# A fp32 two-layer attention and convolution trunk: softmax's division moved into a tanh gate, and another order of the first loads

## The chip, the cores and the metric

The program runs on one core of one Trainium2 chip. The metric is the device time of one execution in microseconds (us). The engines that matter here are TensorE (PE in the rows, with PEld for its weight loads), VectorE (DVE), ScalarE (ACT), GpSimd (POOL) and SyncE (SP), whose queue issues nearly all DMAs.

## What is computed

The input x has 256 tokens of 2048 channels, fp32. Layer 0 is attention, layer 1 a convolution module, and only layer 0 is touched by the change. Cut to what matters:

```
h = x * rsqrt(mean(x*x) + eps) * norm_g          # per token
proj = h @ a_w_in                                # 2048 -> 9*2048 (q, k, v of 3 groups) + 2048 (z)
for each group g of 3, head of 16:
    q, k = q * rsqrt(mean(q*q)) * q_gain, k * rsqrt(mean(k*k)) * k_gain
    s = q k^T / sqrt(128) + bias[bucket(distance), head], masked by the group's window
    o_g = softmax(s) v,   lse_g = log-sum-exp of s
o = sum over g of softmax(lse)_g * o_g           # = one softmax over the three groups' scores
y = o * silu(z)                                  # silu(z) = z / (1 + exp(-z))
x = x + y @ a_w_out
```

As the three groups are merged by their log-sum-exp, one softmax over 512 columns of scores (256 of group 0, 128 each of groups 1 and 2) per token and head gives o. Then comes layer 1 (input projection, gated convolution over 31 taps, layer norm, output projection), and the residual.

## The kernel before, in words

**Weights.** Everything is fp32, computed as three products of fp32r halves: each operand is split into a high part (`hi`, `xh`) and the rest (`lo`, `xl`), and hi·hi, lo·hi and hi·lo are summed in PSUM. The weights come as 480 chunks of 128x1024 (512 KB). `stage(n)` (L101) issues the DMA of chunk n on SP's queue into `raw`, has ScalarE write `hi` and VectorE (or GpSimd, `low_engine`) write `lo`; `raw`, `hi` and `lo` have five buffers each. The main loop (L814) stages chunk n + 3 (`LEAD`), multiplies chunk n, and then runs what `at(n, ...)` had entered for step n. So each engine's program order is that of the steps: chunk n + 3's split, then the helpers of step n.

**Layer 0's projection.** Chunks 0 to 319 go through `project` (L246): 12 matmuls of 512 columns each, the three products of a 128-row block one after the other for token half b = 0 and then b = 1. Eight chunks make one column group (a 512-wide accumulator for each token half), five groups make a set of two heads (`hs`, 8 sets): q and k of the three attention groups, then v, then v and z.

**The first loads.** `load_x(c)` (L140) loads two 128-row blocks of x (256 KB), writes `xh` on ScalarE and `xl` on VectorE, and sums squares on GpSimd: a product (L158) and one or two sums (L160 to L163) per pair of blocks. It is called before `stage` for chunks 0 to 7, all on SP's queue. `warm_up` (L165) runs 16 transposes of an identity and one Exp at the start. `first_norm` (step 8) sums the squares over the channels with one-column matmuls (`token_sums`) and makes r0 = rsqrt(mean).

**Attention.** The helpers of a set run beside the next set's chunks. With e the set's last step: `z_take` at e + 1 copies z (scaled by r0), `z_gate` at e + 2 and e + 3 (token halves) makes z / (1 + exp(-z)) with an Exp on ScalarE and an addition, a reciprocal and a product on VectorE; `z_turn` and `z_put` at e + 4 and e + 5 transpose and copy it. Four units (head, token half) start at t = e + 3, e + 6, e + 9 and e + 12: `scores` at t, `softmax` (bias, maximum, Exp with its sum) at t + 1, `weigh` at t + 2 (reciprocal of the sum on VectorE, then GpSimd multiplies the 128x512 `pr` by it), `turn` at t + 3 (four transposes of `pr` into PSUM), `split` at t + 4 (hi and lo halves of it). Each head's second unit is followed by `values` (t + 5), `gated` (t + 6) and `y_split` (t + 7). The last set has t = e + 1, e + 3, e + 5, e + 7, beside the first chunks of the output projection (`project_out`, 24 matmuls of 256 columns a chunk), where GpSimd writes `lo`. The PSUM tag "t" has two buffers; `scores` (its second half), `turn`, `qk_turn`, `z_turn` and the bias rows take them in turn, each waiting until the one two earlier has been read.

**Bias rows.** In set 0, four times, `bias_load`, `bias_split`, `bias_rows` (two halves) and `bias_store` at steps 8, 10, 11, 12 and 13 (then each 6 later) compute the relative bias and write it to DRAM by SP's queue. The store waits there for VectorE's sum, and the next `bias_load` overwrites the same row buffer.

Of the kernel before, what the change touches and what calls it, by code (L numbers as in the profile page):

```python
# [17 lines left out]
P = 128  # L18
# [23 lines left out]
def hybrid_kernel(ctx: ExitStack, tc: tile.TileContext, x_perm, x_nat, vecs, rel, onehot, maskrow,  # L42
# [85 lines left out]
    yh = bpool.tile([P, NH, S], F32R, tag="yh", name="yh")  # L128
    yl = bpool.tile([P, NH, S], F32R, tag="yl", name="yl")
# [6 lines left out]
    nr0 = cpool.tile([P, 2], F32, name="nr0")  # L136
    gqk = cpool.tile([P, NG], F32, name="gqk")
    ssx = apool.tile([P, S], F32, name="ssx")

    def load_x(c):  # L140

        xr = apool.tile([P, 2, S], F32, tag=("sc", "pr")[c % 2], name=f"xr{c}", bufs=2)
        if c == 0:
            stage(0, 2)
            nc.sync.dma_start(xr[:, 0:1], x_perm[:, 0:1, :])
            nc.sync.dma_start(vec[:, :V_HEAD], vecs[:, :V_HEAD])
        else:
            nc.sync.dma_start(xr, x_perm[:, c * 2:(c + 1) * 2, :])
        for i in range(2):
            k = c * 2 + i  # L150
            if k == 1:
                nc.sync.dma_start(xr[:, 1:2], x_perm[:, 1:2, :])
            g0 = vec[:, V_G0 + k:V_G0 + k + 1]
            nc.scalar.activation(xh[:, k, :], xr[:, i, :], AF.Copy, scale=g0)  # L154
            nc.vector.scalar_tensor_tensor(xl[:, k, :], xr[:, i, :], g0, xh[:, k, :].bitcast(F32),  # L155
                                           op0=ALU.mult, op1=ALU.subtract)
        sq = apool.tile([P, 2, S], F32, tag="sq", name=f"xsq{c}", bufs=2)
        nc.gpsimd.tensor_tensor(sq, xr, xr, op=ALU.mult)  # L158
        if c == 0:
# [86 lines left out]
    def project(n):  # L246
# [146 lines left out]
    def values(st, h):  # L393
# [20 lines left out]
    def gated(st, h):  # L414
# [5 lines left out]
        nc.vector.tensor_tensor(st.y, st.y, st.gz[:, h, :, :], op=ALU.mult)  # L420

    def y_split(st, h):
# [3 lines left out]
        hi = yh[:, head, :].rearrange("p (i f) -> p f i", f=4)  # L426
        lo = yl[:, head, :].rearrange("p (i f) -> p f i", f=4)
# [486 lines left out]
```

## Time and profile before

| | us |
|---|---|
| median of 3 runs (range) | 1473.94 (1473.72 to 1475.07) |
| the profiled execution's own time | 1472.46 |
| its span, first to last instruction | 1470.7 |
| TensorE busy in it | 1448.6 |
| VectorE, ScalarE, GpSimd busy | 988.7, 721.6, 493.2 |

The page's lines by engine give busy times as shares of the span; the waits name who released an engine that sat idle; the timeline gives instructions in order of time, in us from the span's start. A busy time of TensorE is modelled and its matmuls overlap, so the pace is read from the distance of their starts.

### The profile page before, as it was taken

What the parts mean: (1) busy time and instruction counts of PE and PEld (TensorE: products, weight loads), DVE (VectorE), ACT (ScalarE), POOL (GpSimd) and SP (SyncE); (2) the same over time, 40 slices, a digit from 0 to 9 for tenths busy, and PEclk for the clock granted to TensorE, in tenths of its full rate; (3) what the DMA queues carried; (4) which work ended last, traced back from release to release, by engine and by line L of the source; (5) the groups of instructions that cost most, each with busy time, mean ns of one, the idle gap of its engine ahead of it and who ended that gap; (6) DMA issues with size and microseconds to landing.
All of it is one profiled execution on the core that took longest, in us unless ns stands there. A gap on an engine that the chain in (4) does not pass through costs nothing.

```text
span 1470.7 us, 22547 instructions
## 1 busy us (share of the span) xinstructions
PE 1448.6 (98%) x8556; PEld 1277.8 (87%) x8556; DVE 988.7 (67%) x1542; ACT 721.6 (49%) x1011; POOL 493.2 (34%) x394
## 2 busy tenths in 40 slices
PE   8999999999999999999999999999999999999999
PEld 6778888888788888888878888889999999999999
DVE  8656765775675676577567567655658989998621
ACT  5444554454454455445445445544544545455732
POOL 7210220210030022021003002207316979998544
PEclk9999999999999999999999999999999999999999
DMA  7458457457456645745745664566465655555544
GB/s 254 156 185 261 153 188 215 147 170 223 162 160 194 198 154 184 217 150 167 224 159 166 190 201 149 186 170 228 158 201 166 201 180 172 184 190 175 185 161 140
DMA packets 108124, 269.20 MB, mean 183 GB/s; under 512 B 42352, under 2 KB 44656, under 8 KB 108016
## 3 DMA queue, kind: packets, MB, share of 16 engines
q1 hardware_dynamic: 108016, 267.76, 57.6%
q8 instruction: 67, 1.10, 0.3%
q14 instruction: 41, 0.34, 0.1%
HBM read 265.36 MB, written 2.36 MB: 182 GB/s over the span
## 4 chain that ended last, share of the span: by engine, by line
PE 93%; DVE 2%; POOL 2%; ACT 1%; DMA 1%; issue 1%; SPq 0%; ACTq 0%; POOLq 0%; DVEq 0%
PE acc L257 19%; PE acc L259 19%; PE acc L258 18%; PE b L508 6%; PE b L509 6%; PE b L510 6%; PE psq L294 1%; POOL pr L377 1%; ACT hi L109 1%; DMA raw<-w_in 1%; PE vo L510 1%; PE vo L509 1%; PE vo L508 1%; PE vow L496 1%; PE vow L495 1%; PE vow L493 1%
## 5 line engine op out<-in xcount | busy, mean ns | idle before, releaser
L109 ACT CAST hi<-raw 128x1024 fp32r<-128x1024 f32 (+1 forms) x481 | 497.4, 1045 | 297.5 <-PE acc L258 165.3
L110 DVE TENSOR_TENSOR lo<-raw,hi 128x1024 fp32r<-128x1024 f32 (+1 forms) x360 | 444.3, 1238 | 275.6 <-ACT hi L109 267.6
L257 PE MATMUL acc<-hi,xh 128*128 128x512 f32 x1280 | 509.6, 398 | 0.8 <-ACT xh L154 0.8
L259 PE MATMUL acc<-lo,xh 128*128 128x512 f32 x1280 | 501.9, 392 | 3.5 <-DVE lo L110 3.5
L258 PE MATMUL acc<-hi,xl 128*128 128x512 f32 x1280 | 499.7, 390 | 0.4 <-DVE xl L155 0.4
L110 POOL TENSOR_TENSOR lo<-raw,hi 128x1024 fp32r<-128x1024 f32 x121 | 292.8, 2440 | 112.5 <-ACT hi L109 94.6
L259 PEld LDWEIGHTS acc<-lo,xh 128*128 128x128 f32 x1280 | 240.9, 188 | 58.2 <-DVE lo L110 5.7
L257 PEld LDWEIGHTS acc<-hi,xh 128*128 128x128 f32 x1280 | 241.0, 188 | 49.7 <-issue 2.1
L258 PEld LDWEIGHTS acc<-hi,xl 128*128 128x128 f32 x1280 | 241.4, 189 | 48.2 <-DVE xl L155 0.9
L377 POOL TENSOR_SCALAR pr<-pr,m 128x512 f32<-128x512 f32 x32 | 48.7, 1521 | 549.3 <-ACT hi L109 388.0
L508 PE MATMUL b<-hh,hi 128*128 128x256 f32 x768 | 217.8, 284 | 0.0
L509 PE MATMUL b<-hl,hi 128*128 128x256 f32 x768 | 217.3, 283 | 0.0
L510 PE MATMUL b<-hh,lo 128*128 128x256 f32 x768 | 217.3, 283 | 0.0
L655 DVE SCALAR_TENSOR_TENSOR c<-u,vec,c 128x256 f32<-128x256 f32 x464 | 187.5, 482 | 3.5 <-ACT c L651 3.5
L509 PEld LDWEIGHTS b<-hl,hi 128*128 128x128 f32 x768 | 147.4, 192 | 0.0
L508 PEld LDWEIGHTS b<-hh,hi 128*128 128x128 f32 x768 | 147.4, 192 | 0.0
L510 PEld LDWEIGHTS b<-hh,lo 128*128 128x128 f32 x768 | 147.4, 192 | 0.0
L123 POOL TENSOR_SCALAR rq<-ss 128x4 f32<-128x4 f32 x48 | 10.8, 226 | 223.5 <-DVE ss L276 220.7
L371 ACT ACTIVATE pr<-sc,m 128x512 f32<-128x512 f32 x32 | 23.2, 725 | 116.6 <-DVE m L369 116.6
L305 ACT CAST qk<-psq 128x256 fp32r<-128x256 f32 x48 | 17.9, 372 | 76.7 <-PE psq L294 76.7
L307 DVE TENSOR_TENSOR qk<-psq,qk 128x256 fp32r<-128x256 f32 x48 | 20.3, 423 | 49.2 <-ACT qk L306 49.1
L124 POOL TENSOR_TENSOR rq<-rq,nhalf 128x4 f32<-128x4 f32 x48 | 48.4, 1008 | 4.0
(171 smaller groups left out, 1728.6 us busy)
## 6 DMA issues: line engine op xcount, KB each, us to landing
raw<-w_in SPq DMA_DIRECT2D x319, 512.0 KB, 4.2
raw<-v_in SPq DMA_DIRECT2D x96, 512.0 KB, 3.4
raw<-w_out SPq DMA_DIRECT2D x32, 512.0 KB, 3.4
raw<-v_out SPq DMA_DIRECT2D x32, 512.0 KB, 3.9
bt<-btab SPq DMA_DIRECT2D x64, 128.0 KB, 5.2
x<-x_nat SPq DMA_DIRECT2D x4, 512.0 KB, 6.6
out_t<-ob SPq DMA_DIRECT2D x16, 128.0 KB, 1.8
xr<-x_perm SPq DMA_DIRECT2D x7, 256.0 KB, 6.6
```

What stands on the lines that cost most here:

```text
L109: nc.scalar.copy(hi[:, sl], raw[:, sl])
L110: low_engine(n).tensor_tensor(lo[:, sl], raw[:, sl], hi[:, sl].bitcast(F32), op=ALU.subtract)
L124: nc.gpsimd.tensor_tensor(dst, dst, nhalf[:, :n], op=ALU.pow)
L257: nc.tensor.matmul(acc[b], lhsT=xh[:, k, sl], rhs=wh, start=k == 0, stop=False)
L258: nc.tensor.matmul(acc[b], lhsT=xl[:, k, sl], rhs=wh, start=False, stop=False)
L259: nc.tensor.matmul(acc[b], lhsT=xh[:, k, sl], rhs=wl, start=False, stop=k == KT - 1)
L371: nc.scalar.activation(u.pr.rearrange("p a b -> p (a b)"), sc, AF.Exp, bias=u.m[:, 1:2], accum_out=u.m[:, 2:3])
L377: nc.gpsimd.tensor_scalar(pr, pr, u.m[:, 3:4], 0.0, op0=ALU.mult, op1=ALU.add)
L508: nc.tensor.matmul(acc, lhsT=wh, rhs=mh[:, k, :], start=k == 0, stop=False)
L509: nc.tensor.matmul(acc, lhsT=wh, rhs=ml[:, k, :], start=False, stop=False)
L510: nc.tensor.matmul(acc, lhsT=wl, rhs=mh[:, k, :], start=False, stop=k == KT - 1)
L655: nc.vector.scalar_tensor_tensor(c[t % 2], u[:, t:t + S], vec[:, cw + t:cw + t + 1], c[t % 2], op0=ALU.mult, op1=ALU.add)
```

## The change

Two parts. In the first loads, the x blocks of chunk 0 and the first vectors are issued on ScalarE's queue beside the weights on SP's, and the warm-up has 20 transposes. GpSimd's squares are gone: a copy of x with tokens on partitions (`x_tok`, 4 loads of 512 KB, issued in steps 4 to 7 on SP's queue) is squared in place and summed by ScalarE (`token_squares`, steps 7 to 10); its buffer is that of `yh`, which is opened later. `first_norm` goes from step 8 to step 11, and set 0's first q and k sums from 9 to 12 (the normalization from 10 to 14). For chunks 0 to 7, `stage` splits x after the weights' high part and before the low part, and `project` runs the three products of both token halves in the order hi·hi, lo·hi, hi·lo, so that `lo` is wanted after four matmuls and not after two. The bias steps go to 10, 12, 13, 14 and 15, every 5.

In attention, z is scaled by r0/2, and the gate is z/2·(1 + tanh(z/2)): one Tanh on ScalarE, one instruction on VectorE. `weigh` no longer multiplies `pr` on GpSimd; VectorE multiplies the head's 128 columns of the gate by the reciprocal. The gate is turned per head (two transposes, at t + 4 of the head's second unit, copied at t + 5), in the last set's first head two steps later. The first six products of `values` become four: high v by all 512 columns, low v by 256.

```diff
-    def stage(n, parts=1):
+    def stage(n):
+        raw, hi, lo = new_chunk(n)
+        if n < 8:
+            xr = load_x(n)
+        nc.sync.dma_start(raw, source(n))
+        nc.scalar.copy(hi, raw)
+        if n < 8:
+            split_x(n, xr)
+        low_engine(n).tensor_tensor(lo, raw, hi.bitcast(F32), op=ALU.subtract)
...
+    def load_first():
+        xr = apool.tile([P, 2, S], F32, tag="sc", name="xr0", bufs=2)
+        raw, hi, lo = new_chunk(0)
+        for i in range(2):
+            sl = slice(i * 512, (i + 1) * 512)
+            nc.sync.dma_start(raw[:, sl], source(0)[:, sl])
+            nc.scalar.dma_start(xr[:, i:i + 1], x_perm[:, i:i + 1, :])
+            if i == 0:
+                nc.scalar.dma_start(vec[:, :V_HEAD], vecs[:, :V_HEAD])
+        warm_up()
+        for i in range(2):
+            sl = slice(i * 512, (i + 1) * 512)
+            nc.scalar.copy(hi[:, sl], raw[:, sl])
+            x_split(i, xr[:, i, :])
+            nc.vector.tensor_tensor(lo[:, sl], raw[:, sl], hi[:, sl].bitcast(F32), op=ALU.subtract)
...
-        sq = apool.tile([P, 2, S], F32, tag="sq", name=f"xsq{c}", bufs=2)
-        nc.gpsimd.tensor_tensor(sq, xr, xr, op=ALU.mult)
-        if c == 0:
-            nc.gpsimd.tensor_tensor(ssx, sq[:, 0], sq[:, 1], op=ALU.add)
-        else:
-            nc.gpsimd.tensor_tensor(sq[:, 0], sq[:, 0], sq[:, 1], op=ALU.add)
-            nc.gpsimd.tensor_tensor(ssx, ssx, sq[:, 0], op=ALU.add)
+    def load_tokens(i):
+        if i == 0:
+            mixed["x"] = bpool.tile([P, 4, D // 2], F32, tag="yh", name="x_tok")
+        nc.sync.dma_start(mixed["x"][:, i, :], x_tok[i])
+    def token_squares(i):
+        xt = mixed["x"][:, i, :]
+        nc.scalar.activation(xt, xt, AF.Square, accum_out=ssx[:, i % 2, i // 2:i // 2 + 1])
...
-        for i in range(16):
+        for i in range(20):
             nc.tensor.transpose(ps[:, (i % 4) * P:(i % 4 + 1) * P], ident, ident)
...
+    for i in range(4):
+        at(4 + i, load_tokens, i)
+        at(7 + i, token_squares, i)
...
-        at(8 + 6 * f, bias_load, f)
...
-        at(13 + 6 * f, bias_store, f)
+        at(10 + 5 * f, bias_load, f)
...
+        at(15 + 5 * f, bias_store, f)
...
+        if n < 8:
+            order.sort(key=lambda x: x[1])
...
-            nc.scalar.activation(zs, acc[b][:, 256:512], AF.Copy, scale=r0[:, b:b + 1])
+            nc.scalar.activation(zs, acc[b][:, 256:512], AF.Copy, scale=r0h[:, b:b + 1])
...
-        nc.scalar.activation(e, zs, AF.Exp, scale=-1.0)
-        nc.vector.tensor_scalar(e, e, 1.0, None, op0=ALU.add)
-        nc.vector.reciprocal(e, e)
-        nc.vector.tensor_tensor(zs, zs, e, op=ALU.mult)
+        nc.scalar.activation(e, zs, AF.Tanh)
+        nc.vector.scalar_tensor_tensor(zs, e, 1.0, zs, op0=ALU.add, op1=ALU.mult)
...
         nc.vector.reciprocal(u.m[:, 3:4], u.m[:, 2:3])
-        pr = u.pr.rearrange("p a b -> p (a b)")
-        nc.gpsimd.tensor_scalar(pr, pr, u.m[:, 3:4], 0.0, op0=ALU.mult, op1=ALU.add)
+        zs = u.set.zs[u.b][:, u.h * P:(u.h + 1) * P]
+        nc.vector.tensor_scalar(zs, zs, u.m[:, 3:4], None, op0=ALU.mult)
...
+            nc.tensor.matmul(po, lhsT=vh[:, cs], rhs=pp[:, i, :, :], start=i == 0, stop=False, skip_group_check=True)
+            nc.tensor.matmul(po[:, P:3 * P], lhsT=vl[:, cs], rhs=pp[:, i, 1:3, :], start=False, stop=False,
+                             skip_group_check=True)
...
+    def z_turn(st, h):
+        st.pz[h] = t_tile(f"pz{st.hs}_{h}")
+        for b in range(2):
+            nc.tensor.transpose(st.pz[h][:, b * P:(b + 1) * P], st.zs[b][:, h * P:(h + 1) * P], ident)
...
             if e == 7:
-                at(e + 1, first_norm)
-                at(e + 2, qk_sums, hs, g)
-            else:
-                at(e + 1, qk_sums, hs, g)
+                at(e + 4, first_norm)
+                e += 4
+            at(e + 1, qk_sums, hs, g)
...
-        at(e + 4 + 2 * last, z_turn, hs)
-        at(e + 5 + 2 * last, z_put, hs)
+                if last and u.h == 0:
+                    t += 2
+                at(t + 4, z_turn, sets[hs], u.h)
+                at(t + 5, z_put, sets[hs], u.h)
```

## Rows read from the trace of the kernel before

**Rows 1.** The page's first part: busy us (share of the span) and instructions.

```profile
span 1470.7 us, 22547 instructions
...
PE 1448.6 (98%) x8556; PEld 1277.8 (87%) x8556; DVE 988.7 (67%) x1542; ACT 721.6 (49%) x1011; POOL 493.2 (34%) x394
```

**Rows 2.** Timeline, TensorE, a stretch without helpers: start, us, instruction.

```profile
115.56 0.39 PE L257 MATMUL acc<-hi,xh 128*128 128x512 f32 x1
...
118.28 0.39 PE L257 MATMUL acc<-hi,xh 128*128 128x512 f32 x1
```

**Rows 3.** TensorE's waits: us in total, times, longest us.

```profile
PE pt L382 <- POOL pr L377: 11.0, 8, 2.0
PE acc L259 <- DVE lo L110: 3.5, 5, 0.7
...
PE psq L294 <- DVE row L219: 0.8, 1, 0.8
```

**Rows 4.** Timeline of set 0's first unit, beside set 1's chunks: TensorE, ScalarE, GpSimd.

```profile
153.70 0.66 PE L382 MATMUL pt<-ident,pr 128*128 128x128 f32 x4 [1.26 <-POOL pr L377]
...
147.59 0.72 ACT L371 ACTIVATE pr<-sc,m 128x512 f32<-128x512 f32 x1 [6.52 <-DVE m L369]
...
150.85 2.80 POOL L377 TENSOR_SCALAR pr<-pr,m 128x512 f32<-128x512 f32 x1 [53.96 <-ACT hi L109]
```

**Rows 5.** Timeline, TensorE, the start: warm-up, starts of chunks 0, 1 and 8, one wait.

```profile
1.41 3.67 PE L169 MATMUL ps_warm<-ident 128*128 128x128 f32 x16 [1.41 <-POOL ident masks.py:199]
5.90 0.80 PE L257 MATMUL acc<-hi,xh 128*128 128x512 f32 x1 [0.82 <-ACT xh L154]
...
11.91 0.63 PE L257 MATMUL acc<-hi,xh 128*128 128x512 f32 x1
...
19.14 0.50 PE L259 MATMUL acc<-lo,xh 128*128 128x512 f32 x1 [0.68 <-DVE lo L110]
...
36.55 0.39 PE L257 MATMUL acc<-hi,xh 128*128 128x512 f32 x1
```

**Rows 6.** Timeline of the same start: ScalarE, GpSimd, VectorE.

```profile
9.30 1.04 ACT L109 CAST hi<-raw 128x1024 fp32r<-128x1024 f32 x1 [1.77 <-DMA raw<-w_in]
10.87 0.91 ACT L154 ACTIVATE xh<-xr,vec 128x256 fp32r<-128x256 f32 x2 [0.52 <-DMA xr<-x_perm]
...
21.71 2.02 POOL L158 TENSOR_TENSOR xsq<-xr 128x512 f32<-128x512 f32 x1
...
10.38 1.23 DVE L110 TENSOR_TENSOR lo<-raw,hi 128x1024 fp32r<-128x1024 f32 x1 [0.47 <-ACT hi L109]
...
22.75 2.14 DVE L155 SCALAR_TENSOR_TENSOR xl<-xr,vec,xh 128x256 fp32r<-128x256 f32 x2
24.82 1.75 DVE L110 TENSOR_TENSOR lo<-raw,hi 128x1024 fp32r<-128x1024 f32 x1
```

**Rows 7.** Groups by line: busy us, mean ns of one, idle before.

```profile
L308 DVE SCALAR_TENSOR_TENSOR qk<-psq,gqk,qk 128x256 fp32r<-128x256 f32 x48 | 22.7, 474 | 0.0
```

**Rows 8.** Stretches of the start: busy us by engine, PEclk, DMA share, GB/s.

```profile
6.00:13.00 7.00, 6.64 (x15) 4.85 (x16) 6.54 (x7) 3.99 (x7) 6.28 (x7) 1.00 0.97 356
...
20.00:37.00 17.00, 14.13 (x58) 10.34 (x57) 17.00 (x15) 7.10 (x8) 12.36 (x11) 1.00 0.65 213
```

**Rows 9.** Timeline, step 55: VectorE's split of the fourth unit, TensorE's next transposes.

```profile
185.53 0.69 DVE L391 TENSOR_TENSOR pp<-pt,pp 128x512 fp32r<-128x512 f32 x1 [0.89 <-ACT pp L390]
...
187.50 0.60 PE L294 MATMUL psq<-ident,qn 128*128 128x128 f32 x4
```

**Rows 10.** Timeline after SP's first bias store: VectorE's `lo` (chunk 18 first), TensorE's chunk 18.

```profile
63.46 2.51 DVE L110 TENSOR_TENSOR lo<-raw,hi 128x1024 fp32r<-128x1024 f32 x2 [3.28 <-ACT hi L109]
...
68.10 0.50 PE L257 MATMUL acc<-hi,xh 128*128 128x512 f32 x1
```

**Rows 11.** Timeline, VectorE, the gate in the last set, beside GpSimd's `lo`.

```profile
998.75 2.39 DVE L337 TENSOR_SCALAR e<-e 128x256 f32<-128x256 f32 x1 [2.20 <-ACT e L336]
```

**Rows 12.** Groups by line: a load of ScalarE's function table.

```profile
L615 ACT ACT_TABLE_LOAD x1 | 1.3, 1283 | 0.0
```

More of the change, by code (lines that the diff above doesn't have):

```diff
@@ L127, in hybrid_kernel, with open_mixed @@
     xl = bpool.tile([P, KT, S], F32R, tag="xl", name="xl")
-    yh = bpool.tile([P, NH, S], F32R, tag="yh", name="yh")
-    yl = bpool.tile([P, NH, S], F32R, tag="yl", name="yl")
+    mixed = {}
+    def open_mixed():
+        mixed["h"] = bpool.tile([P, NH, S], F32R, tag="yh", name="yh")
+        mixed["l"] = bpool.tile([P, NH, S], F32R, tag="yl", name="yl")
     ph1 = ExitStack()
@@ L135, in hybrid_kernel, with x_split @@
     r0 = cpool.tile([P, 2], F32, name="r0")
-    nr0 = cpool.tile([P, 2], F32, name="nr0")
+    r0h = cpool.tile([P, 2], F32, name="r0h")
     gqk = cpool.tile([P, NG], F32, name="gqk")
-    ssx = apool.tile([P, S], F32, name="ssx")
+    ssx = cpool.tile([P, 2, 2], F32, name="ssx")
+    def x_split(k, xr):
+        g0 = vec[:, V_G0 + k:V_G0 + k + 1]
+        nc.scalar.activation(xh[:, k, :], xr, AF.Copy, scale=g0)
+        nc.vector.scalar_tensor_tensor(xl[:, k, :], xr, g0, xh[:, k, :].bitcast(F32), op0=ALU.mult, op1=ALU.subtract)
@@ L251, in project @@
         acc = acc_a[cg]
+        order = [(b, p) for b in range(2) for p in range(3)]
+        if n < 8:
+            order.sort(key=lambda x: x[1])
         for i in range(2):
@@ L254, in project @@
             wh, wl = hi[:, i * 512:(i + 1) * 512], lo[:, i * 512:(i + 1) * 512]
-            for b in range(2):
+            for b, p in order:
                 sl = slice(b * P, (b + 1) * P)
-                nc.tensor.matmul(acc[b], lhsT=xh[:, k, sl], rhs=wh, start=k == 0, stop=False)
-                nc.tensor.matmul(acc[b], lhsT=xl[:, k, sl], rhs=wh, start=False, stop=False)
-                nc.tensor.matmul(acc[b], lhsT=xh[:, k, sl], rhs=wl, start=False, stop=k == KT - 1)
+                nc.tensor.matmul(acc[b], lhsT=(xl if p == 1 else xh)[:, k, sl], rhs=wl if p == 2 else wh,
+                                 start=k == 0 and p == 0, stop=k == KT - 1 and p == 2)
     class Set:
@@ L266, in hybrid_kernel @@
         sets[hs].qk, sets[hs].qn, sets[hs].rq, sets[hs].pq, sets[hs].pp = {}, {}, {}, {}, {}
+        sets[hs].pz, sets[hs].gz = {}, {}
         sets[hs].hs = hs
@@ L425, in y_split, with z_put @@
         src = st.y.rearrange("p b (f i) -> p (b f) i", f=2)
-        hi = yh[:, head, :].rearrange("p (i f) -> p f i", f=4)
-        lo = yl[:, head, :].rearrange("p (i f) -> p f i", f=4)
+        if not mixed:
+            open_mixed()
+        hi = mixed["h"][:, head, :].rearrange("p (i f) -> p f i", f=4)
+        lo = mixed["l"][:, head, :].rearrange("p (i f) -> p f i", f=4)
         nc.scalar.copy(hi, src)
         nc.vector.tensor_tensor(lo, src, hi.bitcast(F32), op=ALU.subtract)
-    def z_turn(hs):
-        ps = bank("o", f"pz{hs}", 1) if hs == NSET - 1 else t_tile(f"pz{hs}")
-        sets[hs].pz = ps.rearrange("p (h b q) -> p h b q", h=2, b=2)
-        for h in range(2):
-            for b in range(2):
-                nc.tensor.transpose(sets[hs].pz[:, h, b, :], sets[hs].zs[b][:, h * P:(h + 1) * P], ident)
-    def z_put(hs):
-        sets[hs].gz = apool.tile([P, 2, 2, P], F32, tag="gz", name=f"gz{hs}", bufs=1)
-        nc.scalar.copy(sets[hs].gz, sets[hs].pz)
+    def z_turn(st, h):
+        st.pz[h] = t_tile(f"pz{st.hs}_{h}")
+        for b in range(2):
+            nc.tensor.transpose(st.pz[h][:, b * P:(b + 1) * P], st.zs[b][:, h * P:(h + 1) * P], ident)
+    def z_put(st, h):
+        st.gz[h] = apool.tile([P, 2, P], F32, tag="gz", name=f"gz{st.hs}_{h}", bufs=2)
+        nc.scalar.copy(st.gz[h].rearrange("p b q -> p (b q)"), st.pz.pop(h)[:, :2 * P])
     for hs in range(NSET):
@@ L473, in hybrid_kernel @@
                 at(t + 5, values, sets[hs], u.h)
-                at(t + 6, gated, sets[hs], u.h)
-                at(t + 7, y_split, sets[hs], u.h)
-        at(e + 4 + 2 * last, z_turn, hs)
-        at(e + 5 + 2 * last, z_put, hs)
+                if last and u.h == 0:
+                    t += 2
+                at(t + 4, z_turn, sets[hs], u.h)
+                at(t + 5, z_put, sets[hs], u.h)
+                at(t + 6 - (last and u.h == 0), gated, sets[hs], u.h)
+                at(t + 7 - (last and u.h == 0), y_split, sets[hs], u.h)
     oacc = {}
```

53 lines of the change are left out of this document (17 added, 36 removed).

## The prediction

> **What bounds the kernel now.** I read the page's busy times first. TensorE is busy 1448.6 us of a span of 1470.7 us, VectorE two thirds, ScalarE half, GpSimd a third [rows 1]. So nothing off TensorE is worth anything by its length; only two things can move the time: TensorE's own work, and the 22 us in which it is idle or runs slowly. The pace of its work comes from the starts: twelve matmuls of a chunk from 115.56 to 118.28, 2.72 us [rows 2]. Then I read TensorE's waits [rows 3]. Half of the idle time, 11.0 us, is one group: `turn` waits eight times for GpSimd's product of `pr` (L377). The next, 3.5 us in five waits, is for `lo` of the first chunks, and one of 0.8 us is for a bias row. Last I read the start: chunk 0 begins at 5.90, chunk 1 at 11.91, chunk 8 at 36.55 [rows 5]. Eight chunks at 2.72 us would have taken 21.8 us; they took 30.65. Those 8.9 us are half slow pace and half waiting, and not all of it is in the list of waits: chunk 0 took 6.01 us, where a chunk takes 2.72, though the column of the granted clock shows 1.00 for 6 to 13 us [rows 8].
>
> **Part 1, the division.** The stall is the same in each set. TensorE reaches the first unit's transposes 1.26 us before `pr` is there (start 153.70) [rows 4]. GpSimd began its product only at 150.85 and took 2.80 us. But the Exp that made `pr` had ended at 148.31 (147.59 + 0.72), 4.1 us before TensorE came to it at 152.44. After the change `turn` waits for the Exp alone, so the wait goes with 4.1 us to spare, and so do the other seven: 11.0 us [rows 3], of which the longest, 2.0, lies in the last set. Next late would be the Exp or its sums, and they do not come later: VectorE loses the gate's addition and reciprocal in the steps ahead.
>
> What it adds: VectorE multiplies 128 columns of the gate 32 times, and joins the gate's sum and product into one instruction, nearest to 0.47 us for 256 columns [rows 7]. Of VectorE's 988.7 us [rows 1] this is no bound in sets 0 to 6. In the last set it may be: there GpSimd writes `lo`, and a 256-column tensor_scalar of the old gate took 2.39 us beside it [rows 11]. I take the new product between 0 and 2.39 us. At 2.39 the gate's new chain in a step is 2.39 + 0.47, still no longer than the old one, which held that same 2.39 us, a reciprocal and a product; so it costs nothing on the path. The Trainium skill, "SBUF — State Buffer", § Who interferes with whom, says that VectorE and GpSimd share one port pair as an exclusive lock, and that tensor_scalar forms and VectorE instructions with two SBUF inputs can be shut out for a whole GpSimd instruction. The 2.39 us agree. By that rule the four new products of the last set could each take a GpSimd instruction's time, which makes the same sum as my upper end.
>
> `turn` of the gate per head has the same transposes in two groups; `values` has the same columns in fewer instructions. Both I leave at nothing. But the gate's turned tile now takes PSUM tag "t" between a unit's `turn` and the next set's `qk_turn`. So at step 55 `qk_turn` must wait for the fourth unit's split, where it waited for something a step older. That split ended at 186.22 and the transposes came at 187.50 [rows 9]: 1.3 us of cover. Cost zero; if the cover goes, see the rivals.
>
> **Part 2, the start.** VectorE is busy 17.00 of 17.00 us from 20 to 37 [rows 8]: it is the bound there. Per chunk it has two `xl` (2.14) and one `lo` (1.75), starting 22.75 and 24.82, beside GpSimd's squares (2.02 for one) [rows 6]. Before the squares got in its way `lo` took 1.23 (at 10.38) [rows 6], and an instruction of the kind of `xl` takes 0.47 elsewhere [rows 7]. The squares are gone from GpSimd, so I take 2 x 0.47 + 1.23 = 2.17 us per chunk. ScalarE has 1.04 + 0.91 = 1.95 [rows 6]. Both are under TensorE's 2.72, so from chunk 2 on TensorE sets the pace, and only chunk 1 counts.
>
> Chunk 1's `hi` starts at 9.30, when its weights land [rows 6]; I leave that time as it is, since DMAs are busy at a share of 0.97 then [rows 8] and no byte ahead of it is gone. `hi` ends at 10.34, the two `xh` at 11.25, the second `xl` at 11.7, `lo` at 12.9. By then four matmuls of chunk 1 are done (the new order); eight are left, 8 x 2.72 / 12 = 1.8 us: chunk 2 at 14.75. Six chunks more, 16.3 us: chunk 8 at 31.05, against 36.55 [rows 5]: 5.5 us.
>
> The warm-up's four transposes more end near 5.9 (16 took 3.67 from 1.41) [rows 5], when chunk 0 begins anyway. Bounds: ScalarE was idle 1.77 us before that `hi` [rows 6], so weights that come sooner, thanks to the x loads on ScalarE's queue, bring at most 1.77 more: 7.2. Downward: if chunk 0's slow pace (6.01 instead of 2.72) also held for chunk 1's last eight matmuls and chunk 2, that costs 3.29 x 20 / 12 = 5.5, and nothing is gained. At full pace or half pace chunk 0 itself does not matter, as it ends before 12.9. I take 5.5, since the rows of chunk 2 before show no slow pace any more (chunk 1's end and 2 to 7 have VectorE as bound).
>
> The bias row's wait of 0.8 us [rows 3] goes, since the bias rows leave the steps of set 0's first `qk_turn`. The squares on ScalarE come in steps 7 to 10, where it has over a microsecond free per step by the 1.95 above; r0 comes three steps later, and the accumulator is still free two steps before column group 2 needs it. SP's queue: the new store and the next bias load are in one step, so the chunk behind them is wanted one chunk (2.72 us) sooner. Before, chunk 18's `lo` ended at 64.69 and it was multiplied at 68.10 [rows 10]: 3.4 us of cover, of which 0.7 is left, in three places. Cost zero, bound 1 us each.
>
> **The sum.** 11.0 + 5.5 + 0.8 = 17.3 us. The profiled execution took 1472.46 us, so 1455.2; the runs' median is 1473.94, 1.5 above the profiled one, and I give the time on the median's scale: 1456.6.
>
> **The rivals.**
> (a) VectorE was slow at the start for another reason than GpSimd. Then `xl` and `lo` keep 2.14 and 1.75, 3.74 us a chunk in turn, and the new order (`xl` before `lo`) puts chunk 1's `lo` at 14.7, chunk 7's at 37.1, chunk 8 at 38.9: 2.4 us lost in place of 5.5 gained. 1472.46 - 11.0 - 0.8 + 2.4 + 1.5 = 1464.5. For it: nothing but that the same lines run 2 us together over many chunks; against it: `lo` at 10.38. Chance 0.10.
> (b) A new wait takes the old one's place: VectorE's product, held up by 2.39 us as in [rows 11], delays the fourth unit's split beyond its 1.3 us of cover [rows 9], 1.1 us in each of 7 sets: 7.7, so 1464.3. Against it: GpSimd has lost its long instructions in those sets. 0.06.
> (c) Tanh needs another function table than Exp. A load takes 1.28 us [rows 12]; two a set hide in ScalarE's 6.5 us of idle time before the Exp [rows 4]. In the last set Tanh and Exp alternate, and two loads could lie ahead of the second `turn`: 2.6, so 1459.2. 0.05. The Trainium skill, "ScalarE: Activation LUTs", § Table sets: the hidden batching unit, lists tanh in Exp's set, which speaks against a load; no run shown here has a Tanh.
> (d) The other sign: x is now read twice. Up to chunk 11, the first behind the last token load, 12 x 512 KB + 8 x 256 KB + 4 x 512 KB, 10.5 MB, must land by 37.0 (chunk 11 is due at 39.2, less 2.3 for `hi` and `lo`): 284 GB/s from the start of the span. 356 GB/s were moved from 6 to 13 us; the 213 of 20 to 37 fall where VectorE was the bound [rows 8]. Below 284 TensorE waits at chunks 8 to 11, below 10.5 MB / 54.3 us = 193 GB/s the whole gain of 17.3 is gone. At 175 GB/s chunk 11 comes 23 us late: 1479.6. 0.04.
>
> **How the numbers follow.** Forecast 0.72, the four rivals 0.25, 0.03 for what I do not see. Predicted is the forecast's 1456.6. Its own range is 1454.0 (the start at 7.2, and the small savings left at nothing) to 1462 (the start at nothing). The range that should hold the time 8 in 10 adds (a), (b) and (c): 1453.5 to 1465.0. A measurement of this kernel can tell about 0.2%, 2.9 us, from no change. Faster by more than that: the forecast, (a), (b), (c), 0.93. Within it 0.03, slower 0.04.
>
> **What would show it.** Right: no wait of `turn` on GpSimd nor anything in its place; `xl` near 0.5 and `lo` near 1.2 us from the start; chunk 8 near 31. Wrong: waits of `qk_turn` on VectorE's split in each set (b), table loads beside Tanh (c), waits of `hi` on weights that TensorE passes on at chunks 8 to 11 (d), `xl` still at 1 us (a), or a slow pace of TensorE beyond 13 us.

## The result and the profile after

| | before | after |
|---|---|---|
| median, us (range) | 1473.83 (1472.41 to 1475.07) | 1452.55 (1452.36 to 1452.66) |
| the profiled execution, its span | 1472.46, 1470.7 | 1452.36, 1450.6 |
| ratio of times (95% interval) | | 0.9856 (0.9841 to 0.9872) |

The change gained 21.3 us. The prediction said 1456.6, range 1453.5 to 1465.0: the sign is right, the time is 1.0 us below the range. One of the four executions of e3 below took 3428.68 us, at a granted clock of 1.00 and for a reason that no trace here shows; e3's time and ratio are those of the other three.

The page's first part after (the line that answers to [rows 1]), then all of TensorE's waits (engine, line, what it waited for: us in total, times, longest), which answer to [rows 3]:

```profile
span 1450.6 us, 22407 instructions
...
PE 1442.3 (99%) x8524; PEld 1275.6 (88%) x8524; DVE 960.2 (66%) x1542; ACT 727.0 (50%) x1027; POOL 423.7 (29%) x339
```

```profile
PE ps_warm L195 <- POOL ident masks.py:199: 1.4, 1, 1.4
PE psq L327 <- DVE qn L319: 1.4, 1, 1.4
PE acc L290 <- DVE lo L117: 0.8, 1, 0.8
PE psq L327 <- DVE row L248: 0.8, 1, 0.8
PE ps_rn L600 <- DVE rn L755: 0.7, 1, 0.7
```

No wait of `turn` is left, of the five waits for `lo` one, the bias row's wait is still there, and one of 1.4 us for `qn` is new (before, one of 0.3 us for `qn` stood in the list). The waits were 11.0 + 3.5 + 0.8 before; but the span fell by 20.1. Where it went is read from four starts of TensorE, in both kernels:

| stretch of TensorE | before | after | difference | forecast |
|---|---|---|---|---|
| to the start of chunk 8 | 36.55 | 29.70 | -6.85 | -5.5 |
| chunks 8 to 39 (set 0) | 98.05 | 98.61 | +0.56 | -0.8 |
| chunks 40 to 319 (7 sets) | 856.53 | 845.27 | -11.26 | -9.0 |
| first half of the output projection (`wow`) | 56.99 | 54.59 | -2.40 | -2.0 |
| the rest | 422.6 | 422.4 | -0.2 | 0 |

The third and fourth line share the forecast's 11.0 us, with the longest wait, 2.0, in the fourth. The sum is -20.1 where -17.3 was forecast.

The timeline of TensorE at the start, after (start, us, instruction; it answers to [rows 5]), shows the first loss removed:

```profile
9.38 0.73 PE L290 MATMUL acc<-hi,xh 128*128 128x512 f32 x2
...
11.43 0.73 PE L290 MATMUL acc<-lo,xh 128*128 128x512 f32 x2 [0.80 <-DVE lo L117]
...
13.38 0.61 PE L290 MATMUL acc<-hi,xh 128*128 128x512 f32 x2
...
29.70 0.39 PE L290 MATMUL acc<-hi,xh 128*128 128x512 f32 x1
```

Chunk 1 begins at 9.38, waits 0.80 for `lo`, and chunk 2 begins at 13.38. From there six chunks take 16.32 us, 2.72 each, the pace of [rows 2]: chunk 8 begins at 29.70. VectorE and ScalarE in the same stretch (to compare with [rows 6]):

```profile
9.36 0.88 DVE L152 SCALAR_TENSOR_TENSOR xl<-xr,vec,xh 128x256 fp32r<-128x256 f32 x2 [1.48 <-ACT xh L151]
10.16 1.22 DVE L117 TENSOR_TENSOR lo<-raw,hi 128x1024 fp32r<-128x1024 f32 x1
...
7.87 1.05 ACT L114 CAST hi<-raw 128x1024 fp32r<-128x1024 f32 x1 [1.11 <-DMA raw<-w_in]
```

Two `xl` take 0.88 and `lo` 1.22, where they took 2.14 and 1.75. And `hi` of chunk 1 begins at 7.87, not at 9.30.

### The profile page after: what moved, and what is told of

It reads as the page before. It is cut to its first block, busy times and chain, and to the rows that moved or that the text cites. A ratio compares the mean times of both kernels' runs of the same rounds, so it can differ in the third digit from the quotient of the medians.

```text
span 1450.6 us, 22407 instructions
## 1 busy us (share of the span) xinstructions
PE 1442.3 (99%) x8524; PEld 1275.6 (88%) x8524; DVE 960.2 (66%) x1542; ACT 727.0 (50%) x1027; POOL 423.7 (29%) x339
## 4 chain that ended last, share of the span: by engine, by line
PE 98%; DMA 1%; DVE 0%; ACT 0%; issue 0%; SPq 0%; POOL 0%; POOLq 0%; ACTq 0%
PE acc L290 60%; PE b L541 6%; PE b L542 6%; PE b L543 6%; PE psq L327 1%; PE wow L526 1%; PE vo L543 1%; PE vo L542 1%; PE vo L541 1%; PE vow L529 1%; PE vow L528 1%; PE vow L526 1%; PE wo L543 1%; PE wo L541 1%; PE wo L542 1%; PE wow L528 1%
## 5 line engine op out<-in xcount | busy, mean ns | idle before, releaser
L114 ACT CAST hi<-raw 128x1024 fp32r<-128x1024 f32 x479 | 497.0, 1048 | 292.7 <-PE acc L290 164.2
L117 DVE TENSOR_TENSOR lo<-raw,hi 128x1024 fp32r<-128x1024 f32 x358 | 441.3, 1234 | 282.2 <-ACT hi L114 275.7
L129 POOL TENSOR_SCALAR rq<-ss 128x4 f32<-128x4 f32 x48 | 10.9, 226 | 789.7 <-DVE ss L309 787.8
L422 ACT CAST pp<-pt 128x512 fp32r<-128x512 f32 x32 | 18.8, 587 | 44.1 <-PE pt L414 42.8
```

Source lines behind the costliest of these rows:

```text
L114: nc.scalar.copy(hi, raw)
L117: low_engine(n).tensor_tensor(lo, raw, hi.bitcast(F32), op=ALU.subtract)
```

## The experiments

The theory going in: `turn` is freed because the Exp alone stands ahead of it; VectorE's start is freed because GpSimd's squares go. Rivals: it is the gate's shorter chain that frees `turn`; the start is faster by its loads or its order. All times are medians in us, with the ratio to before and its 95% interval.

**The parts alone.** e1 is before with the attention part only; e2 is after with the attention part taken back.

```diff
 e1, on before
+        nc.scalar.activation(e, zs, AF.Tanh)
+        nc.vector.scalar_tensor_tensor(zs, e, 1.0, zs, op0=ALU.add, op1=ALU.mult)
...
+        nc.vector.tensor_scalar(zs, zs, u.m[:, 3:4], None, op0=ALU.mult)
...
+                at(t + 4, z_turn, sets[hs], u.h)
 e2, on after
+        nc.scalar.activation(e, zs, AF.Exp, scale=-1.0)
...
+        nc.gpsimd.tensor_scalar(pr, pr, u.m[:, 3:4], 0.0, op0=ALU.mult, op1=ALU.add)
...
+        at(e + 4 + 2 * last, z_turn, hs)
```

> The kernel before with the attention part of the change alone: tanh gate, division moved into it, gate turned per head, fewer value products. By the forecast's own prices (the listed idle time of the eight waits, 11.0 us) the span of the profile falls from 1470.7 to 1459.7 us. By the distance of the starts, a wait costs more than its listed idle time, since TensorE's last matmul before it is counted as busy to a modelled end: 1.49 us instead of 1.28 in each of sets 0 to 6, and the turn of the gate is 0.14 cheaper, so 1.63 us a set and 2.4 in the last one, 13.7 in all: 1457.0 us. The start stays: chunk 8 at 36.55 us.

> The changed kernel with the attention part undone: old gate, GpSimd's division, old turn and value products. The start and the bias steps are those of the change. If the two parts add up, chunk 8 begins at 29.7 us, the eight waits for GpSimd's product are back (1.28 us listed each in seven sets, 2.0 in the last), and the span is 1450.6 + 13.7 = 1464.3 us. If the parts do not add up (a bias row or q/k wait that the attention part shifts), the span departs from that by more than 1 us.

e1: 1458.25, 0.9895 (0.9881 to 0.9910), span 1456.7. e2: 1466.59, 0.9954 (0.9937 to 0.9971), span 1464.0. By spans the parts give 14.0 and 6.7, in sum 20.7 against 20.1 together: they add. A set takes 120.69 in e1 and 122.34 in e2 (122.37 before). e2 has the eight waits of [rows 3] back, listed at 10.9 us where the attention part is worth 14.0 by the spans:

```profile
PE pt L415 <- POOL pr L410: 10.9, 8, 2.0
```

**What freed `turn`.** e3 is after, but GpSimd multiplies `pr` again, ahead of `turn`. e11 is before with the tanh gate alone. e4 is after with the old gate, the division still moved.

```diff
 e3, on after
...
-        nc.vector.tensor_scalar(zs, zs, u.m[:, 3:4], None, op0=ALU.mult)
...
+        nc.gpsimd.tensor_scalar(pr, pr, u.m[:, 3:4], 0.0, op0=ALU.mult, op1=ALU.add)
 e11, on before
...
-        nc.scalar.activation(e, zs, AF.Exp, scale=-1.0)
-        nc.vector.tensor_scalar(e, e, 1.0, None, op0=ALU.add)
-        nc.vector.reciprocal(e, e)
-        nc.vector.tensor_tensor(zs, zs, e, op=ALU.mult)
+        nc.scalar.activation(e, zs, AF.Tanh)
+        nc.vector.scalar_tensor_tensor(zs, e, 1.0, zs, op0=ALU.add, op1=ALU.mult)
 e4, on after
...
-        nc.scalar.activation(e, zs, AF.Tanh)
-        nc.vector.scalar_tensor_tensor(zs, e, 1.0, zs, op0=ALU.add, op1=ALU.mult)
+        nc.scalar.activation(e, zs, AF.Exp, scale=-1.0)
+        nc.vector.tensor_scalar(e, e, 1.0, None, op0=ALU.add)
+        nc.vector.reciprocal(e, e)
+        nc.vector.tensor_tensor(zs, zs, e, op=ALU.mult)
```

> The changed kernel, but GpSimd divides pr as before (the gate is not multiplied); the tanh gate stays. Theory A (the place of the division is what cost): turn waits for GpSimd in each set again, 1.49 us by the starts, 2.4 in the last, span 1450.6 + 12 = 1462.6 us. Theory B (the long gate on VectorE, 2.5 us twice a set, made the sums, the Exp and so the division late; 1.9 us of it lay ahead of the first unit's sums): GpSimd's product ends before TensorE comes to it and there is no wait in sets 0 to 6, span within 2.5 us of 1450.6.

> The kernel before with the tanh gate alone: GpSimd still divides pr, the gate is turned once a set, the start and all else are as before. If VectorE's long gate is the cause of turn's wait (GpSimd's product is only late because VectorE's sums and the Exp ahead of it were late), all eight waits go: 1.49 us by the starts in seven sets, some 2.3 in the last, span 1470.7 - 12.7 = 1458.0 us. If the division's place is the cause, the waits stay and the span is near 1470.

> The changed kernel with the old gate (Exp, sum, reciprocal, product on VectorE) but the division in the gate, so that turn waits for the softmax's Exp alone. If moving the division is enough by itself, as the forecast argued (the Exp of the kernel before ended 4.1 us before TensorE came to it), there is no wait of turn and the span is within 1 us of 1450.6, though VectorE has some 35 us more work. If the long gate also delays something else that TensorE waits for, the span is longer by 1 us or more.

e3: 1452.74, 0.9858 (0.9842 to 0.9874), span 1450.6 as after, and no wait of `turn` at all. e11: 1460.12, 0.9911 (0.9897 to 0.9926), all eight waits gone as well. So the move of the division was not needed: the tanh gate does it alone. Timelines say why. Before, VectorE (start, us, instruction), ahead of set 0's first unit:

```profile
142.04 0.29 DVE L337 TENSOR_SCALAR e<-e 128x256 f32<-128x256 f32 x1
142.36 1.75 DVE L338 RECIPROCAL e<-e 128x256 f32<-128x256 f32 x1
144.15 0.42 DVE L339 TENSOR_TENSOR zs<-zs,e 128x256 f32<-128x256 f32 x1
144.49 1.22 DVE L110 TENSOR_TENSOR lo<-raw,hi 128x1024 fp32r<-128x1024 f32 x1
145.63 0.42 DVE L364 TENSOR_TENSOR sc<-s,bt 128x256 f32<-128x256 f32 x1
```

e11, the same unit, VectorE, ScalarE, GpSimd:

```profile
143.31 0.42 DVE L363 TENSOR_TENSOR sc<-s,bt 128x256 f32<-128x256 f32 x1 [0.99 <-PE s L350]
...
145.37 0.72 ACT L370 ACTIVATE pr<-sc,m 128x512 f32<-128x512 f32 x1 [4.30 <-DVE m L368]
...
148.62 1.76 POOL L376 TENSOR_SCALAR pr<-pr,m 128x512 f32<-128x512 f32 x1 [51.82 <-ACT hi L109]
```

TensorE's scores of this unit start at 142.76 in both. Before, the softmax's first sum began at 145.63, behind addition, reciprocal, product and `lo`; in e11 at 143.31, when the scores are there. So the Exp begins 2.2 us sooner, and GpSimd's product 2.2 us sooner (148.62 against 150.85 [rows 4]); it also takes 1.76 and not 2.80. It ends at 150.38, before TensorE comes to it (152.28, the last matmul's 152.05 and one pace).

e4: 1456.12, 0.9877 (0.9862 to 0.9892), span 1454.3. A set takes 120.75, as after: the move of the division also frees seven waits alone. So in seven places of eight either half of the change is enough, and neither is the one cause of those waits. In the last set the move alone is not enough. e4, VectorE and TensorE there:

```profile
990.36 2.27 DVE L370 TENSOR_SCALAR e<-e 128x256 f32<-128x256 f32 x1 [2.14 <-ACT e L369]
...
995.79 0.92 PE L415 MATMUL pt<-ident,pr 128*128 128x128 f32 x4 [2.11 <-DVE pp L424]
```

Beside GpSimd's `lo` the gate's addition takes 2.27 (0.29 in the sets), `split` of the first unit stands behind the gate, and the next `turn` waits 2.11 us for that. Then the clock falls. Stretches of e4 before and behind that wait (from:to and us; busy us of PE, PEld, DVE, ACT, POOL; granted clock, DMA share, GB/s):

```profile
990.00:996.00 6.00, 3.89 (x34) 3.69 (x33) 5.54 (x6) 1.74 (x4) 4.77 (x2) 1.00 0.32 102
996.10:999.40 3.30, 3.30 (x18) 3.30 (x17) 1.80 (x5) 1.34 (x3) 0.00 (x0) 0.50 0.39 145
```

The granted clock is 0.50, 1.2 GHz, through the second stretch (by the trace's clock record from 996.05 to 999.46, 3.4 us); the half projection takes 58.45 where it takes 54.59 after: 3.9 us, 2.1 for the wait and 1.7 for the half clock. e4's four executions fit: 1454.71 at a mean granted clock of 1.000, and 1456.08 to 1456.49 at 0.998 to 0.999.

**VectorE at the start.** e6 is after, with GpSimd's squares of x back beside ScalarE's (their sums are used by nothing).

```diff
...
+        squares(c, xr)
...
+        nc.gpsimd.tensor_tensor(sq, xr, xr, op=ALU.mult)
...
+            nc.gpsimd.tensor_tensor(sq[:, 0], sq[:, 0], sq[:, 1], op=ALU.add)
+            nc.gpsimd.tensor_tensor(ssq, ssq, sq[:, 0], op=ALU.add)
```

> The changed kernel with GpSimd's squares and sums of x added back beside the first loads (their result is used nowhere). If they are what made VectorE slow at the start, xl takes near 1.07 us and lo near 1.75 again, 3.74 us a chunk, chunk 8 begins near 37 us in place of 29.7, and the span is near 1458. If VectorE's pace had another cause (rival a), xl stays at 0.48, lo at 1.22, and the span at 1450.6.

e6: 1460.27, 0.9908 (0.9891 to 0.9924). Chunk 8 starts at 37.35, 7.65 us later than after; the span is 7.8 longer. VectorE, and TensorE's waits:

```profile
20.32 2.14 DVE L153 SCALAR_TENSOR_TENSOR xl<-xr,vec,xh 128x256 fp32r<-128x256 f32 x2
22.38 1.75 DVE L117 TENSOR_TENSOR lo<-raw,hi 128x1024 fp32r<-128x1024 f32 x1
```

```profile
PE acc L302 <- DVE lo L117: 6.2, 7, 1.8
```

The durations of before are back to the hundredth [rows 6]. GpSimd's squares were the cause, and their removal is more than the start's whole gain: with them, the rest of the start's change brings chunk 8 0.8 us later than before (37.35 against 36.55).

**The first loads.** e5 is after, with x of chunk 0 and the vectors issued on SP's queue behind chunk 0's weights.

```diff
-            nc.scalar.dma_start(xr[:, i:i + 1], x_perm[:, i:i + 1, :])
+        for i in range(2):
+            nc.sync.dma_start(xr[:, i:i + 1], x_perm[:, i:i + 1, :])
             if i == 0:
-                nc.scalar.dma_start(vec[:, :V_HEAD], vecs[:, :V_HEAD])
+                nc.sync.dma_start(vec[:, :V_HEAD], vecs[:, :V_HEAD])
```

> The changed kernel with the first x loads and the first vectors back on SP's queue behind the two halves of chunk 0. The forecast's theory (chunk 1's weights land when the bytes ahead of them are through, so the queue does not matter): chunk 2 at 13.4 us as in the changed kernel, span 1450.6. Rival theory (they land a fixed time after SP issues them, and three issues less on SP are 1.4 us: 3.52 to 2.09 issue, 9.28 to 7.85 landing): landing near 9.3, chunk 2 near 14.8, span 1452.0.

e5: 1455.07, 0.9875 (0.9860 to 0.9889). SP's issue of chunk 1's weights after (2.09):

```profile
2.09 0.43 SPq L113 DMA_DIRECT2D raw<-w_in  x1
```

In e5 (3.52), with ScalarE and TensorE behind it:

```profile
3.52 0.43 SPq L113 DMA_DIRECT2D raw<-w_in  x1
...
9.29 1.04 ACT L114 CAST hi<-raw 128x1024 fp32r<-128x1024 f32 x1 [2.71 <-DMA raw<-w_in]
...
10.80 0.74 PE L291 MATMUL acc<-hi,xh 128*128 128x512 f32 x2 [1.84 <-ACT xh L151]
...
12.86 1.22 PE L291 MATMUL acc<-lo,xh 128*128 128x512 f32 x2 [0.81 <-DVE lo L117]
...
16.44 1.05 PE L291 MATMUL acc<-hi,xh 128*128 128x512 f32 x2
```

Three issues of 0.48 us stand ahead, the weights are issued 1.43 us later, and `hi` begins 1.42 later (9.29 against 7.87): one for one. In the profiled execution more followed, in the stretches of e5:

```profile
6.00:11.00 5.00, 3.16 (x13) 1.94 (x13) 2.00 (x5) 2.29 (x5) 0.00 (x0) 1.00 0.93 313
12.00:18.70 6.70, 5.88 (x15) 4.59 (x15) 5.80 (x10) 6.23 (x10) 0.00 (x0) 0.50 0.96 354
```

About 1.2 us behind the wait of 1.84 the granted clock falls to 0.50, 1.2 GHz (by the trace's clock record from 11.97 to 18.80, so ahead of the wait of 0.81), and chunk 8 begins at 33.87: 4.17 late for 1.42 of cause. That execution is the longest of four; by the medians e5 loses 2.5.

**The warm-up and the order.** e7 is after with 16 warm-up transposes; e9 is after with the old order of the products.

```diff
 e7
-        for i in range(20):
+        for i in range(16):
 e9
-            order.sort(key=lambda x: x[1])
+            pass
```

> The changed kernel with 16 transposes in the warm-up in place of 20, so that TensorE is idle for some 0.7 us before chunk 0, as in the kernel before. If the idle time ahead of chunk 0 is why TensorE ran chunk 0 at half pace there (0.43 us between starts of 512 columns, in place of 0.23), chunk 0 takes over 5 us again and chunk 2 begins near 14.5 in place of 13.4: span 1451.7. If the pace had another cause, chunk 0 stays at 3.6 us and the span at 1450.6.

> The changed kernel with the old order of products in chunks 0 to 7 (lo wanted after two matmuls of a chunk, not four). In chunk 1 TensorE waits for lo until 11.4 us in both; with the old order ten matmuls are left then and not eight, 2 x 0.227 = 0.45 us: chunk 2 at 13.85 and the span 1451.1. If lo arrives ahead of need the order does nothing: 1450.6.

e7: 1453.07, 0.9859 (0.9845 to 0.9874); chunk 2 at 13.29. e9: 1452.92, 0.9863 (0.9848 to 0.9878); chunk 2 at 14.11, with `lo` waited for 1.04 us instead of 0.80. Both differ from after by about 0.5 or less, under the bound of 2.9: neither the four transposes nor the order carries a gain that the times show. In the profiled execution of e9 chunk 8 comes at 30.43, 0.73 later than after, so the order may be worth up to that. e7 begins chunk 0 after an idle 0.68, and still needs 3.56 us for it:

```profile
5.73 0.73 PE L290 MATMUL acc<-hi,xh 128*128 128x512 f32 x2 [0.68 <-ACT xh L151]
...
9.29 0.74 PE L290 MATMUL acc<-hi,xh 128*128 128x512 f32 x2 [0.19 <-ACT xh L151]
```

**The bias steps.** e8 is after with the bias steps at 9, 11, 12, 13 and 14, every 6. A store and the next load are then not in one step, and all the bias steps fall elsewhere against the q and k steps.

```diff
-        at(10 + 5 * f, bias_load, f)
+        at(9 + 6 * f, bias_load, f)
...
-        at(15 + 5 * f, bias_store, f)
+        at(14 + 6 * f, bias_store, f)
```

> The changed kernel with the bias steps at 9, 11, 12, 13 and 14, every 6 steps, so that a store and the next load stand one step apart and no bias row falls in the steps of group 2's q/k turns. The forecast priced the new bias steps at nothing; by it the span stays at 1450.6 us. By the trace of the changed kernel, TensorE waits 1.39 us in step 27 (for the normalized q and k, which stand on VectorE behind a low part whose weights SP issued late, behind the store) and 0.77 us in step 28 (behind a bias row): without them the span is 1450.6 - 2.5 = 1448.1 us.

e8: 1450.09, 0.9839 (0.9824 to 0.9854), span 1448.4, 2.2 less than after. Both waits of `psq` are gone; but for the warm-up's 1.4 there are left:

```profile
PE acc L290 <- DVE lo L117: 0.8, 1, 0.8
PE ps_rn L600 <- DVE rn L755: 0.7, 1, 0.7
```

How the waits came about stands in the timeline of after: SP's queue, ScalarE, VectorE, TensorE.

```profile
85.14 0.31 SPq L230 DMA_DIRECT2D row<-maskrow  x1
85.51 2.62 SPq L113 DMA_DIRECT2D raw<-w_in  x5
...
89.31 1.05 ACT L114 CAST hi<-raw 128x1024 fp32r<-128x1024 f32 x1 [7.25 <-DMA raw<-w_in]
...
90.40 1.23 DVE L117 TENSOR_TENSOR lo<-raw,hi 128x1024 fp32r<-128x1024 f32 x1 [4.90 <-ACT hi L114]
91.54 1.28 DVE L319 TENSOR_TENSOR qn<-acc,rq 128x512 f32<-128x512 f32 x2
...
92.28 0.66 PE L327 MATMUL psq<-ident,qn 128*128 128x128 f32 x4 [1.39 <-DVE qn L319]
```

The store is issued at 83.20, the row's next load waits behind it in SP's queue for the store's end, and the weights issued at 85.51 are the next that ScalarE gets: it has stood idle for 7.25 us. TensorE did not miss the chunk itself. But its `lo` stands in VectorE's queue ahead of `qn`, whose inputs from GpSimd were done at 87.02 and 88.75, and `qk_turn` waits for `qn`.

e8 doesn't bring that chunk sooner. ScalarE and VectorE there:

```profile
90.39 1.05 ACT L114 CAST hi<-raw 128x1024 fp32r<-128x1024 f32 x1 [8.20 <-DMA raw<-w_in]
...
89.17 0.69 DVE L319 TENSOR_TENSOR qn<-acc,rq 128x512 f32<-128x512 f32 x1 [1.04 <-POOL rq L312]
```

ScalarE stands idle even longer, 8.20 us, but the late `lo` (91.47) now comes behind both `qn`. So the place in VectorE's queue is what e8 mended; whether a store and a load one step apart would have been enough by itself isn't shown.

**What was left.** e10 is e8 with chunks 1 and 2 loaded and split in halves, so that chunk 1 is not one unit of hi, `xh`, `xl` and `lo`. e12 is e10 with x of chunk 1 issued on ScalarE's queue.

```diff
 e10, on e8
+        if n in (1, 2):
+            for i in range(2):
+                sl = slice(i * 512, (i + 1) * 512)
+                nc.sync.dma_start(raw[:, sl], source(n)[:, sl])
+            for i in range(2):
...
+                nc.scalar.copy(hi[:, sl], raw[:, sl])
+                x_split(n * 2 + i, xr[:, i, :])
+                nc.vector.tensor_tensor(lo[:, sl], raw[:, sl], hi[:, sl].bitcast(F32), op=ALU.subtract)
+            return
...
 e12, on e10
...
+        nc.scalar.dma_start(early["x"], x_perm[:, 2:4, :])
...
```

> The kernel of e8_bias_steps with chunks 1 and 2 loaded and split in two halves of 512 columns, as chunk 0 is. Chunk 1's wait for lo (0.8 us listed, after a pause of 0.5 us before the chunk) is for a split of 1024 columns; by the half, lo of the first half comes about 1 us sooner and chunk 2 begins near 12.2 in place of 13.4 us: span 1447.2. If the weights' landing bounds it (one issue more on SP), nothing is gained: 1448.4.

> As e10_halves, with the x blocks of chunk 1 issued on ScalarE's queue too, so that SP issues chunk 1's weights one slot (0.47 us) sooner. If the landing follows the issue on SP, chunk 1's weights land 0.4 us sooner than in e10_halves, span 0.4 lower; if ScalarE's later table load and first high part (0.45 us of issue more ahead of them) come later than TensorE wants them, chunk 0 begins later and the span is 0.3 higher.

e10: 1448.80 (1448.69 to 1448.87), 0.9834 (0.9818 to 0.9851), span 1447.1. Chunk 1's wait for `lo` is gone and chunk 2 begins 1.36 us sooner than after:

```profile
12.02 0.61 PE L300 MATMUL acc<-hi,xh 128*128 128x512 f32 x2
```

This is the best version, 3.75 us under after and 25 under before. e12: 1449.24, 0.9837 (0.9823 to 0.9852): chunk 1's first half of weights lands at 6.58 instead of 7.33, chunk 2 begins at 11.87, 0.15 sooner, and the time is 0.4 longer: too little to be told from no change. What it gains at chunk 2 it loses at chunk 5, whose weights land at 16.91 instead of 16.40; chunk 8 begins at 28.71 instead of 28.42.

## Why the prediction was right in sign and too high

**Part 1, 11.0 us of waits: the waits went, but they were priced too low, and half of the cause was missed.** They are gone, with 5.7 us to spare (`pr` ready at 139.79, transposes at 145.50) where 4.1 was forecast.

The reason: the prediction put the stall on GpSimd's product standing between the Exp and `turn`, and taking it away is indeed enough in seven places of eight (e4). e3 and e11 show what it missed: 2.46 us of gate (addition, reciprocal, product) stood in VectorE's queue ahead of the softmax sums and made that product late. In its own sentence the prediction noted that VectorE "loses the gate's addition and reciprocal in the steps ahead", but counted on it only so that nothing new would come late. The shorter gate is enough in all eight places. In the eighth, the move alone left a wait of 2.11 us for VectorE's `split` behind the old gate.

The price is the step that failed: a listed wait counts from the modelled end of the matmul before it, and that end lies 0.39 us behind its start, while the next may start 0.23 behind it [rows 2]. By starts, a set's wait is worth more than the 1.26 listed in [rows 4]. TensorE, before and after:

```profile
152.05 0.39 PE L259 MATMUL acc<-lo,xh 128*128 128x512 f32 x1
```

```profile
145.26 0.40 PE L290 MATMUL acc<-lo,xh 128*128 128x512 f32 x1
145.50 0.60 PE L414 MATMUL pt<-ident,pr 128*128 128x128 f32 x4
```

From the last product to the transposes it was 1.65 us (152.05 to 153.70), and is 0.24. That makes 1.4 for this unit, and over a set it agrees with e11, where only the gate changed: 120.87 against 122.37, 1.50 a set. Seven sets of 1.50 are 10.5, not 9.0. The remaining 0.12 a set between e11 and after, 0.8 in seven, came with the rest of part 1, priced at nothing. It is not the move of the division, since e3, without it, has 120.75 as well; the turn per head or the fewer products of `values` are left. The half projection gained 2.40, not 2.0.

**VectorE's product in the last set** was bounded between 0 and 2.39. In its four places there it took 2.23, 1.64, 1.26 and 1.25 (0.29 in the sets). The gate's one instruction, taken at 0.47, took 2.58 and 2.42 there. So the chain in a step was 2.58 + 2.23, not 0.47 + 2.39, and no shorter than the old gate (2.27 + 1.75 + 0.68 in e4's last set); but none of TensorE's waits is for it:

```profile
142.19 0.29 DVE L409 TENSOR_SCALAR zs<-zs,m 128x128 f32<-128x128 f32 x1
...
983.83 2.23 DVE L409 TENSOR_SCALAR zs<-zs,m 128x128 f32<-128x128 f32 x1
```

The Trainium skill's page "SBUF — State Buffer", § Who interferes with whom, has VectorE and GpSimd share one port pair. The runs agree: with GpSimd at work, `lo` took 1.75 for 1.22, two `xl` 2.14 for 0.88 and the old addition 2.27 for 0.29; GpSimd's own product took 2.80 before and 1.76 in e11 (0.70 in e11's last set).

**Part 2, 5.5 us: 6.85 came.** The cause was right (e6), and so were 2 x 0.47 + 1.23 per chunk (0.88 + 1.22) and six chunks in 16.3. The step that was mis-sized is one sentence: "I leave that time as it is, since DMAs are busy at a share of 0.97". Chunk 1's `hi` began at 7.87, 1.43 sooner, by exactly the issue time that left SP's queue (e5), and all that hangs on it came sooner: chunk 2 at 13.38 instead of 14.75, the whole 1.37 of the miss. The share of 0.97 was no ceiling. After, in the stretch of [rows 8]:

```profile
6.00:13.00 7.00, 6.07 (x23) 4.23 (x24) 5.52 (x10) 5.68 (x10) 0.00 (x0) 1.00 1.02 393
```

393 GB/s moved where 356 had, at a share of 1.02. The bound of 1.77 us that the prediction named for this held; the value inside it was wrong. On a queue per engine the Trainium skill, "DMA: Bandwidth & Descriptors", § Issuing engines are not separate DMA queues, says that only the time of issuing is saved, usually small beside the transfer; here that time, 1.43 us, was all there was to gain.

**The bias steps, -0.8 forecast, +0.56 measured.** Two steps failed. The old wait for a bias row did not go: one of 0.77 is there at step 28. And the delay behind the store was priced at zero, bound 1 us, by the cover of the delayed chunk in [rows 10]. That cover held. The prediction asked only when the chunk is wanted by TensorE; what had none was the work that stands behind the chunk's `lo` in VectorE's queue. e8, without both waits, is 2.2 us shorter.

**The scale, +1.5.** The sum against the profiled execution was 1455.2; with the table's four deviations (-1.35 for the start, -2.66 for the waits, +1.36 for the bias steps, -0.15 for the rest) it is 1452.4, and the profiled execution took 1452.36. The step up to the median, 1.5 before, is 0.2 after. Of 22 executions of before with a listed clock, eleven at a mean granted clock of 1.000 average 1472.95 us and eleven at 0.997 to 0.999 average 1474.18. After, e8, e10 and e11, which have no `turn` wait, list 1.000 in all four, though e1 and e6, which have none either, list 0.999 once and twice (e6's at 1460.16 and 1460.34, no longer than its others); e2, which has all eight, lists 0.999 twice (1467.17, 1467.57) and 1.000 twice (1465.77, 1466.01). So about 1.3 us of the gain look like a clock that no longer falls behind a stall, as e4's trace shows one. That before's falls behind the same stalls was not caught in a profile: this is argued, not shown, and the cause of the 1.3 us stays open. With the step of 1.5 the time would have been 1453.9, inside the range by 0.4; so the time left it by this term together with the price of the waits and of the start.

**The rivals.** (a), slow for another reason: refuted by e6. Its price was 1.6 too high: with slow VectorE and the new order chunk 8 came at 37.35 (38.9 forecast), 0.8 lost and not 2.4. (b), a new wait on the "t" bank: no wait of `qk_turn` on `split` is in the list. (c), table loads: a Tanh takes 0.42 us and no load stands beside it; the only load of ScalarE's table by then is the first one, at 2.12. The Trainium skill, "ScalarE: Activation LUTs", § Table sets: the hidden batching unit, has tanh and exp in one set, and the trace agrees. (d), not enough bandwidth: 284 GB/s were needed, and 380 moved from 20 to 37 us; none of TensorE's waits is on a load. Chunk 0's slow pace, kept as a bound of 5.5 us, did not reach past it: after, full pace (0.23 us from start to start) begins at 6.8.

## What to carry to other kernels

Ask of a stall not only who released it, but what stood in that engine's queue ahead of the releaser: the named product on GpSimd was 2.2 us late because a long gate stood ahead of the softmax sums on VectorE, and shortening that was enough, as was, in seven places of eight, taking the product off the path. Price a wait by the starts around it in both directions, and a delayed load by everything that stands behind its consumers in their queues, not by its own due time. At a kernel's start count the issue time on the queue: here it moved a landing one for one (1.43 and 1.42 us) although the DMA share was near 1.

## What the runs showed of the hardware

- The granted clock of TensorE fell to 0.50 (1.2 GHz) behind a wait of 2.11 us (e4, for 3.4 us) and behind one of 1.84 us (e5, for 6.8 us), which took the price of the first to 3.9 us and that of e5's later landing from 1.42 to 4.17. It did not behind eight waits of up to 2.0 us in the profiled execution of before.
- At the start TensorE runs at half pace for a while, though the granted clock's column shows 1.00 [rows 8]. The timeline of before has it in chunk 0, 0.43 us from start to start, until 12.8 us (0.23 later). The trace's clock record begins only there, at 12.80, and at 6.78 after, where the half pace ends too: ahead of it the column's 1.00 stands for no record and not for a granted clock. 0.43 us is also e5's pace at a granted 0.50, so the start looks like the 1.2 GHz level. Two starts of before:

```profile
8.07 0.63 PE L257 MATMUL acc<-hi,xh 128*128 128x512 f32 x1
8.50 0.63 PE L258 MATMUL acc<-hi,xl 128*128 128x512 f32 x1
```

In the other kernels full pace began between 4.9 us (e7, with 16 transposes) and 10.4 us (e1, whose loads and warm-up are those of before); in e11, with the same loads and warm-up, by 5.7. So the number of transposes doesn't order them. What does is left open.
